# Runs of 1 to 16 small two-byte products between the tiles of the gate and up projection

## The chip, the cores and the metric

The kernel runs on one core of one Trainium2 chip. The metric is the device time of one execution in microseconds (us), smaller being better.

## The reference, cut to what matters

The reference is two transformer blocks on 256 tokens of width 1024. The first block has a mixer (latent attention beside a gated linear recurrence), a gated feed-forward layer and a gated embedding; the second has two attentions and a layer that picks experts by product keys. The change lies in the feed-forward layer of the first block:

```python
D_MODEL = 1024
D_FF = -(-8 * D_MODEL // (3 * 256)) * 256      # 2816
...
h = rms_norm(x, g_ffn[l])
x = x + (jax.nn.silu(h @ w_gate[l]) * (h @ w_up[l])) @ w_down[l]
gate = jax.nn.sigmoid(rms_norm(x, g_ple[l]) @ w_ple_gate[l])
x = x + gate * (p[l].astype(x.dtype) @ w_ple_proj[l])
```

`w_gate` and `w_up` are 1024 x 2816 each. The kernel holds them as one array `w_gu` of 44 units of 128 columns, a gate unit and an up unit in turn.

## The kernel before

**One product in three.** Weights and activations are float32, and each is split into a high part (`whi`, `hh`, of type fp32r) and a low rest (`wlo`, `hl`). A product is then the sum of three: high by high, high by rest, rest by high. `mm3s` (line 120) issues them: for one tile of `w_gu` it has 8 pieces of the inner dimension and three products of each, so 24 products of 128 x 128 weights with 256 tokens, 8 of each kind in a row, all added up in one PSUM bank of the pool `mm` (three buffers).

**One unit of weights.** `unit` (line 98) loads 512 KB of weights on SP's queue into `wraw`, ScalarE (ACT) rounds them to `whi` (L109), and VectorE (DVE) subtracts to get `wlo` (L114). `wraw`, `whi` and `wlo` have four buffers each, so the splits may run up to four units ahead of TensorE (PE).

**The tile loop.** `prodT` (line 133) walks over the units. For each 128 columns it takes a PSUM bank, calls `mm3s`, and then `emit` for the tile. With `pre` (here the two steps of the norm, `sums` at L234 and `spread` at L241, small products with `ones` and `ident`) the first emits are held back until the norm is there. `w_gu` is one call of `prodT` with 44 units. `emit_gu` scales a tile by the norm (L786, DVE); for a gate tile it takes SiLU (L789, ACT), and for an up tile it multiplies the two (L792, DVE) and splits the result into `acth` (L180, ACT) and `actl` (L181, DVE), which feed the products of `w_down` behind: 8 tiles of 66 products each. After these come the 48 products of `w_ple_proj`.

**The order.** The kernel is written for a tile framework that orders the instructions of each engine while it builds the program, from its own costs; each engine then runs its own list in order and waits on semaphores. PE, ACT, DVE, POOL (GpSimd) and SP have a list each.

**Another place with small products.** The experts' weights of the second block are spread to a table by products of one-hot float16 tiles (L1221): 8 or 16 products of 128 x 128 with 128 columns at a time, and between two such groups stand 24 wide products of L129, the same shape as a tile of `w_gu`.

Of the kernel before, what the change touches and what calls it, by code (L numbers as in the profile page):

```python
# [10 lines left out]
BF16 = mybir.dt.bfloat16  # L11
# [52 lines left out]
def body(tc, a, out, dbg=None):  # L64
    nc = tc.nc
    ctx = ExitStack()
    pool = lambda name, bufs=1, **k: ctx.enter_context(tc.tile_pool(name=name, bufs=bufs, **k))
# [8 lines left out]
    G = nc.gpsimd  # L76
    PE = nc.tensor

    def pmm():
        return ps.tile([128, 512], F32, name="mm", bufs=3)  # L80
# [4 lines left out]
    def tick(n):  # L85

        for g in list(sides):
            for _ in range(n):
                if next(g, "end") == "end":
                    sides.remove(g)  # L90
                    break
# [6 lines left out]
    def unit(ap, shape, pool=False, parts=1, between=None):  # L98


        n = int(np.prod(shape))
        raw = st.tile([128, 1024], F32, name="wraw", bufs=4)
        hi = st.tile([128, 1024], F32R, name="whi", bufs=4)
        lo = st.tile([128, 1024], F32R, name="wlo", bufs=4)
        ap = ap.rearrange("p a b -> p (a b)")
        for i in range(parts):
            s = slice(i * n // parts, (i + 1) * n // parts)
            nc.sync.dma_start(raw[:, s], ap[:, s])
            S.activation(hi[:, s], raw[:, s], AF.Copy)  # L109
            if pool == "add":  # L110
                S.activation(lo[:, s], raw[:, s], AF.Copy, scale=-1.0)
                G.dma_start(lo[:, s], raw[:, s], accum_op=OP.add)
            else:
                (G if pool else V).tensor_tensor(lo[:, s], raw[:, s], hi[:, s].bitcast(F32), op=OP.subtract)  # L114
            if between is not None:
                between(i)
        v = lambda t: t[:, :n].rearrange("p (a b) -> p a b", a=shape[0])
        return v(hi), v(lo)

    def mm3s(o, steps, x_late=False, fill=None, first=True, last=True):  # L120


        if x_late:
            order = [(i, j) for i in range(len(steps)) for j in range(3)]
        else:
            order = [(i, j) for j in (0, 2, 1) for i in range(len(steps))]
        for n, (i, j) in enumerate(order):
            wh, wl, xh, xl = steps[i]
            PE.matmul(o, (wh, wl, wh)[j], (xh, xh, xl)[j], start=first and n == 0, stop=last and n == len(order) - 1)  # L129
            if fill is not None and j == 2 and i < len(steps) - 1:  # L130
                fill()

    def prodT(name, n0, n1, kt, cols, x, emit, steps=0, pool=lambda u: False, pre=(), given=None, fill=None, behind=(), late=False):


        xh, xl = x
        held = []
        late = late or len(pre) > 0
        pre = list(pre)
        for u in range(n0, n1):  # L140
            wh, wl = given if given is not None and u == n0 else unit_behind(behind if u > n0 + 1 else (), a[name][u], (kt, cols), pool(u))
            for c in range(cols // 128):
                p = pmm()
                o = p[:, :T]
                s = slice(c * 128, (c + 1) * 128)
                first = late and u == n0 and c == 0
                mm3s(o, [(wh[:, k, s], wl[:, k, s], xh[:, k], xl[:, k]) for k in range(kt)], first, fill if first else None)
                held.append((u * (cols // 128) + c, o))
                if pre:
                    pre.pop(0)()  # L150
                if not pre:
                    for i in held:
                        emit(*i)
                    held = []
                tick(steps)

    def natural(p, wh, wl, x, j, kts, first, last, x0=0):
# [21 lines left out]
    def split(hi, lo, src):  # L179
        S.activation(hi, src, AF.Copy)  # L180
        V.tensor_tensor(lo, src, hi.bitcast(F32), op=OP.subtract)  # L181
# [6 lines left out]
    def unit_behind(behind, *args, **kw):  # L188

        with ExitStack() as order:  # L190
            for i in behind:
                order.enter_context(tc.issue_after(i.ins))
            return unit(*args, **kw)
# [54 lines left out]
    def show(name, ap):  # L248
        if dbg is not None and name in dbg:
            nc.sync.dma_start(dbg[name], ap)  # L250
# [22 lines left out]
    with tc.tile_pool(name="la", bufs=1) as la, tc.tile_pool(name="pa", bufs=1, space=PSUM) as pa:  # L273
# [425 lines left out]
        steps = nm1.make(pay)  # L699
# [8 lines left out]
        def emit_gz(j, p):  # L708
# [4 lines left out]
            G.tensor_tensor(gz[:, j], gz[:, j], rows[:, 128:640], op=OP.mult)  # L713

        prodT("w_in", 0, 4, 8, 128, h, emit_z, 4, pre=[steps[0], first_spread], given=unit0, pool=lambda u: u == 2, fill=busy)
        sides.append(tables())
        latent_stats()
        prodT("w_in", 4, 10, 8, 128, h, emit_z, 3, pool=lambda u: u > 4 and u % 2 == 1 and "add")
        ready.add(("z", 0))
        sides.extend([hgrn(), hgrn_out()])  # L720
# [19 lines left out]
        for j in range(2):  # L740
# [3 lines left out]
            S.activation(vm[:, j], pv, AF.Copy, scale=rc[:, 1, j:j + 1])  # L744
        sides.append(mla_k(pk))
        prodT("w_in", 10, 16, 8, 128, h, emit_z, 1, pool=lambda u: u % 2 == 1 and "add")
        ready.add(("z", 1))
        nat512("w_in_nat", 4, h, emit_gz, 4, pool=lambda q: q % 2 == 1 and "add")
# [28 lines left out]
    with tc.tile_pool(name="lf", bufs=1) as la, tc.tile_pool(name="pf", bufs=1, space=PSUM) as pf:  # L777
        pfx = lambda: pf.tile([128, 512], F32, name="fx", bufs=2)
        n1 = norm
        act = (la.tile([128, 22, T], F32R, name="acth"), la.tile([128, 22, T], F32R, name="actl"))  # L780
        hold = {}

        def emit_gu(n, o):
            f, up = n // 2, n % 2
            t = la.tile([128, T], F32, name=f"gu{up}", bufs=2)
            V.tensor_tensor(t, o, n1.r, op=OP.mult)  # L786
            if up == 0:
                s = la.tile([128, T], F32, name="gsi", bufs=2)
                S.activation(s, t, AF.Silu)  # L789
                hold[0] = s  # L790
            else:
                V.tensor_tensor(t, t, hold[0], op=OP.mult)  # L792
                split(act[0][:, f], act[1][:, f], t)

        prodT("w_gu", 0, 44, 8, 128, n1.h, emit_gu, pre=n1.make(pfx), behind=n1.last)
        x2 = xb()
        norm2 = Norm("g_ple")
        for n in range(8):
            p = pmm()
            for k0, k1 in ((0, 8), (8, 16), (16, 22)):  # L800
                wh, wl = unit(a["w_down"][n][:, k0:k1], (k1 - k0, 128))
                mm3s(p[:, :T], [(wh[:, k], wl[:, k], act[0][:, k0 + k], act[1][:, k0 + k]) for k in range(k1 - k0)],
                     n == 0 and k1 == 22, first=k0 == 0, last=k1 == 22)
            V.tensor_tensor(x2[:, n], x1[:, n], p[:, :T], op=OP.add)
            norm2.add(n, x2[:, n])
        show("x2", x2)

        pT = la.tile([128, 2, T], F32, name="pT")
        nc.sync.dma_start(pT, a["pT"])
        pR = (la.tile([128, 2, T], F32R, name="pRh"), la.tile([128, 2, T], F32R, name="pRl"))  # L810
        split(pR[0], pR[1], pT)
        pp = la.tile([128, 8, T], F32, name="pp")

        def emit_pp(n, o):
            S.activation(pp[:, n], o, AF.Copy, scale=0.5)

        prodT("w_ple_proj", 0, 2, 2, 512, pR, emit_pp)
        x3 = xa()
        norm = Norm("g_mix2")

        def emit_ple(n, o):
            t = la.tile([128, T], F32, name="gu0", bufs=2)
            V.tensor_tensor(t, o, norm2.r, op=OP.mult)
            S.activation(t, t, AF.Tanh, scale=0.5)
            V.scalar_tensor_tensor(t, t, 1.0, pp[:, n], op0=OP.add, op1=OP.mult)
            V.tensor_tensor(x3[:, n], x2[:, n], t, op=OP.add)
            norm.add(n, x3[:, n])

        prodT("w_ple_gate", 0, 8, 8, 128, norm2.h, emit_ple, pre=norm2.make(pfx), behind=norm2.last)
        show("x3", x3)  # L830
# [595 lines left out]
```

## Time and profile before

| | us |
|---|---|
| median of 3 runs | 1429.27 |
| lowest and highest of these | 1424.44 and 1433.63 |
| the profiled execution, its own time | 1428.57 |
| its span, first to last instruction | 1426.8 |

The profile is that of one execution. PE is the time of products, PEld that of loading their stationary operand, which overlaps. A row of the timeline gives the start, the time from the first start to the last end, the engine, the line, the operation, the tiles, the shape and how many instructions are merged in it; in brackets stands the idle time before it and what ended that. A product's own time is longer than the distance between two starts, since products overlap in the array; what a stream of products costs is read from the starts. Some product records are missing from the trace, so counts in a window can be a few per cent low.

### The profile page before, as it was taken

The page shows a single profiled execution, that of the slowest core. Times are in us where ns is not written, and L with a number is a line of the kernel's source. Part 1 is how long each engine was busy: PE and PEld are TensorE (multiplying, and loading weights), DVE is VectorE, ACT ScalarE, POOL GpSimd, SP SyncE. Part 2 cuts the span into 40 slices and gives each one's busy share as a digit, 9 for nine tenths or more (in the row PEclk, how much of TensorE's full clock was granted, in tenths as well). Part 3 has the DMA queues.
Part 4 walks back from the last instruction along what each step waited for, and adds up shares of the span by engine and source line. Part 5 has one row for each costly group of instructions (what it writes and reads, how often), then busy time and mean ns, then how long its engine had stood idle before and what let it go on. Part 6 is the DMA issues. An engine that isn't in the chain of part 4 may idle for free.

```text
span 1426.8 us, 25304 instructions
## 1 busy us (share of the span) xinstructions
PE 1396.8 (98%) x9962; PEld 1281.2 (90%) x9962; DVE 961.2 (67%) x1792; ACT 770.3 (54%) x1183; POOL 127.6 (9%) x118
## 2 busy tenths in 40 slices
PE   9899999999999999989999999999999999999997
PEld 9796899999979889989999999989999899888886
DVE  7866876666775557776978995655555555577775
ACT  6764655444655444654358885444445444444443
POOL 4322200001110000147300000000000000000000
PEclk9999999999999999999999999999999999999999
DMA  7662466566555334664468778777667776797652
GB/s 242 193 176 61 156 201 185 191 178 192 165 166 155 112 118 148 204 179 153 133 210 291 269 277 289 217 218 218 196 208 220 217 220 201 234 277 224 205 191 89
DMA packets 105143, 277.52 MB, mean 195 GB/s; under 512 B 8512, under 2 KB 42048, under 8 KB 102848
## 3 DMA queue, kind: packets, MB, share of 16 engines
q1 hardware_dynamic: 100848, 252.31, 56.9%
q10 hardware_dynamic: 2304, 16.78, 2.8%
q0 software_dynamic: 1872, 6.82, 2.6%
q8 instruction: 78, 1.28, 0.4%
q14 instruction: 41, 0.34, 0.1%
HBM read 251.23 MB, written 17.83 MB: 189 GB/s over the span
## 4 chain that ended last, share of the span: by engine, by line
PE 86%; DVE 4%; DMA 4%; ACT 2%; issue 2%; POOL 1%; POOLq 0%; SPq 0%; ACTq 0%; DVEq 0%
PE mm L129 47%; PE ax L1249 8%; PE ax L1251 8%; PE ax L1250 8%; PE mm L163 4%; PE ax L1221 2%; PE mm L1057 2%; DMA wlo<-wraw 1%; PE sc L919 1%; DVE wlo L114 1%; PE sc L129 1%; ACT whi L109 1%; PE ao L913 1%; DMA gd<-hl 1%; DMA wraw<-in_expert_u_dram 0%
## 5 line engine op out<-in xcount | busy, mean ns | idle before, releaser
L109 ACT ACTIVATE whi<-wraw 128x1024 fp32r<-128x1024 f32 (+3 forms) x445 | 456.8, 1031 | 479.5 <-PE mm L129 154.9
L114 DVE TENSOR_TENSOR wlo<-wraw,whi 128x1024 fp32r<-128x1024 f32 (+3 forms) x410 | 486.9, 1191 | 262.2 <-ACT whi L109 252.8
L129 PE MATMUL mm<-hh,whi 128*128 128x256 f32 x1912 | 279.5, 285 | 1.2 <-DVE xa L766 0.7
L129 PE MATMUL mm<-hh,wlo 128*128 128x256 f32 x1912 | 268.9, 280 | 6.5 <-DMA wlo<-wraw 3.6
L129 PE MATMUL mm<-hl,whi 128*128 128x256 f32 x1912 | 269.7, 280 | 1.2 <-DVE hl L186 1.0
L129 PEld LDWEIGHTS mm<-hh,whi 128*128 128x128 f32 x1912 | 249.9, 189 | 8.9 <-ACT whi L109 0.9
L129 PEld LDWEIGHTS mm<-hh,wlo 128*128 128x128 f32 x1912 | 242.7, 189 | 7.3 <-DMA wlo<-wraw 3.8
L129 PEld LDWEIGHTS mm<-hl,whi 128*128 128x128 f32 x1912 | 242.6, 189 | 2.3 <-DVE hl L186 2.2
L1249 PE MATMUL ax<-whi,al 128*128 128x512 f32 x512 | 202.8, 396 | 1.5 <-DVE al L181 1.5
L1251 PE MATMUL ax<-whi,ah 128*128 128x512 f32 x512 | 202.6, 396 | 0.0
L1250 PE MATMUL ax<-wlo,ah 128*128 128x512 f32 x512 | 202.3, 395 | 0.0
L1251 PEld LDWEIGHTS ax<-whi,ah 128*128 128x128 f32 x512 | 96.2, 188 | 23.0
L1249 PEld LDWEIGHTS ax<-whi,al 128*128 128x128 f32 x512 | 96.2, 188 | 22.0 <-issue 1.7
L1250 PEld LDWEIGHTS ax<-wlo,ah 128*128 128x128 f32 x512 | 96.3, 188 | 20.4
L1062 ACT ACTIVATE hs<-mm 128x256 f32<-128x256 f32 x128 | 47.5, 371 | 45.5 <-PE mm L129 28.6
L1265 POOL TENSOR_TENSOR ff<-fss 128x1 f32<-128x1 f32 x2 | 1.4, 700 | 723.3 <-ACT fsq L1260 723.3
L114 POOL TENSOR_TENSOR wlo<-wraw,whi 128x1024 fp32r<-128x1024 f32 x22 | 52.8, 2400 | 39.7 <-ACT whi L109 33.6
L181 DVE TENSOR_TENSOR al<-am,ah 128x256 fp32r<-128x256 f32 x128 | 53.4, 418 | 0.0
L180 ACT ACTIVATE ah<-am 128x256 fp32r<-128x256 f32 x128 | 51.4, 401 | 3.6 <-DVE am L1238 3.6
L786 DVE TENSOR_TENSOR gu<-mm,rbc 128x256 f32<-128x256 f32 x44 | 18.6, 424 | 39.4 <-PE mm L129 39.4
L1211 DVE TENSOR_TENSOR one<-iota,iab 128x2048 f16<-128x2048 f16 x32 | 39.0, 1220 | 2.0 <-PE ax L1221 2.0
L1214 DVE TENSOR_TENSOR oA<-one,g 128x2048 f16<-128x2048 f16 x32 | 39.1, 1225 | 1.0
(406 smaller groups left out, 1558.7 us busy)
## 6 DMA issues: line engine op xcount, KB each, us to landing
wraw<-in_expert_u_dram SPq DMA_DIRECT2D x128, 512.0 KB, 4.1
wraw<-in_expert_v_dram SPq DMA_DIRECT2D x128, 512.0 KB, 3.6
wraw<-in_w_gu_dram SPq DMA_DIRECT2D x44, 512.0 KB, 3.5
wraw<-in_w_in_nat_dram SPq DMA_DIRECT2D x24, 512.0 KB, 3.5
wraw<-in_w_down_dram SPq DMA_DIRECT2D x16, 512.0 KB, 3.6
wraw<-in_w_in_g_dram SPq DMA_DIRECT2D x16, 512.0 KB, 3.5
wraw<-in_w_pq_dram SPq DMA_DIRECT2D x16, 512.0 KB, 4.6
gd<-hh ACTq DMA_DIRECT2D x8, 1024.0 KB, 6.7
```

Of the source, the lines that this page charges most:

```text
L109: S.activation(hi[:, s], raw[:, s], AF.Copy)
L114: (G if pool else V).tensor_tensor(lo[:, s], raw[:, s], hi[:, s].bitcast(F32), op=OP.subtract)
L129: PE.matmul(o, (wh, wl, wh)[j], (xh, xh, xl)[j], start=first and n == 0, stop=last and n == len(order) - 1)
L163: PE.matmul(p, xs[:, x0 + k, s], w[:, k], start=first and i == 0 and k == 0, stop=last and i == 2 and k == kts - 1)
L180: S.activation(hi, src, AF.Copy)
L181: V.tensor_tensor(lo, src, hi.bitcast(F32), op=OP.subtract)
L1062: S.activation(t, p[:, :T], AF.Gelu)
L1211: V.tensor_tensor(one, iota[:, None].to_broadcast(s2), iab[:, qs].rearrange("p q w b -> p (q w) b")[:, :, None].to_broadcast(s2), op=OP.is ...
L1214: V.tensor_tensor(A2, ow[:, :, 0:1].to_broadcast(s3), g2[:, qs].rearrange("p q k b -> p (q k) b")[:, :, None].to_broadcast([128, PAIRS * 2 ...
L1249: PE.matmul(o, al[:, js], hi[:, ns], start=c == 0, stop=False)
L1250: PE.matmul(o, ah[:, js], lo[:, ns], start=False, stop=False)
L1251: PE.matmul(o, ah[:, js], hi[:, ns], start=False, stop=c == 127)
```

## The change

`prodT` gets a callback `then` that is called after each tile. In the call for `w_gu` it puts a run of small products on PE: each is a product of a bfloat16 tile of ones, 128 x 128, with itself, into 128 columns of a PSUM bank of its own (`between`, of the pool `fx`), which nothing reads. The table `runs` has one number for each of the 44 tiles: 28 of them are not zero, and they sum to 190.

```diff
-    def prodT(name, n0, n1, kt, cols, x, emit, steps=0, pool=lambda u: False, pre=(), given=None, fill=None, behind=(), late=False):
+    def prodT(name, n0, n1, kt, cols, x, emit, steps=0, pool=lambda u: False, pre=(), given=None, fill=None, behind=(), late=False, then=None):
...
                     held = []
+                if then is not None:
+                    then()
                 tick(steps)
...
-        prodT("w_gu", 0, 44, 8, 128, n1.h, emit_gu, pre=n1.make(pfx), behind=n1.last)
+        onesb = la.tile([128, 128], BF16, name="onesb")
+        G.memset(onesb, 1.0)
+        between = pfx()
+        runs = [0, 0, 1, 0, 2, 0, 3, 0, 4, 0, 5, 0, 6, 0, 7, 0, 8, 0, 9, 0, 10, 0, 11, 0, 12, 0, 8, 8, 12, 12, 4, 4, 1, 1, 2, 2, 3, 3, 16, 0, 8, 16, 12, 0]
+
+        def run_of_ones():
+            for _ in range(runs.pop(0)):
+                PE.matmul(between[:, 0:128], onesb, onesb, start=True, stop=True)
+
+        prodT("w_gu", 0, 44, 8, 128, n1.h, emit_gu, pre=n1.make(pfx), behind=n1.last, then=run_of_ones)
```

The built programs show where the new instructions stand. Lines behind the new code are higher by 2 or by 11 in the changed kernel. The first place is PE's list at the start of `w_gu`, from the second tile's step of the norm on; before it reads:

```order
L129 MATMUL mm<-hh,wlo 128x256 x8
L241 MATMUL fx<-cst,rnat 128x128 x2
L129 MATMUL mm<-hh,whi 128x256 x8
L129 MATMUL mm<-hl,whi 128x256 x8
L129 MATMUL mm<-hh,wlo 128x256 x8
L129 MATMUL mm<-hh,whi 128x256 x8
```

and in the changed kernel, from the second of these tiles to the second run:

```order
L129 MATMUL mm<-hh,wlo 128x256 x8
L804 LDWEIGHTS onesb
L804 MATMUL fx<-onesb 128x128
L129 MATMUL mm<-hh,whi 128x256 x8
L129 MATMUL mm<-hl,whi 128x256 x8
L129 MATMUL mm<-hh,wlo 128x256 x8
L129 MATMUL mm<-hh,whi 128x256 x8
L129 MATMUL mm<-hl,whi 128x256 x8
L129 MATMUL mm<-hh,wlo 128x256 x8
L804 LDWEIGHTS onesb
L804 MATMUL fx<-onesb 128x128
```

Each small product is a load of weights and a product of its own; the wide products around it keep their order, and the list has 190 such pairs in all.

The second place is POOL's list around the end of the mixer. `onf` belongs to the mixer's last norm, and `sqa` and `rnat` to the norm ahead of `w_gu`; before:

```order
L713 TENSOR_TENSOR gz<-gz,rows 128x512 x2
L198 TENSOR_TENSOR onf_1676<-onf_1677,mhalf 128x4
L198 TENSOR_TENSOR onf_1694<-onf_1695,mhalf 128x4
L223 TENSOR_TENSOR sqa<-sq 128x256
L223 TENSOR_TENSOR sqa<-sqa,sq 128x256 x5
```

and in the changed kernel:

```order
L715 TENSOR_TENSOR gz<-gz,rows 128x512 x2
L200 TENSOR_TENSOR onf_1676<-onf_1677,mhalf 128x4
L200 TENSOR_TENSOR onf_1694<-onf_1695,mhalf 128x4
L798 MEMSET onesb 128x128
L225 TENSOR_TENSOR sqa<-sq 128x256
L225 TENSOR_TENSOR sqa<-sqa,sq 128x256 x5
```

The memset of `onesb` went in ahead of the norm's sums. Its memory belonged to tiles of the mixer, so it waits for them, the last being the mixer's transposes on PE (L533 before).

The third place is DVE's list at the 28th tile of `w_gu`, from where on the two programs differ to near the end of the loop; before:

```order
L181 TENSOR_TENSOR actl<-gu_2994,acth 128x256
L786 TENSOR_TENSOR gu_3065<-mm,rbc 128x256
L114 TENSOR_TENSOR wlo<-wraw,whi 128x1024
L792 TENSOR_TENSOR gu_3065<-gu_3065,gsi 128x256
L786 TENSOR_TENSOR gu_3101<-mm,rbc 128x256
L114 TENSOR_TENSOR wlo<-wraw,whi 128x1024
L181 TENSOR_TENSOR actl<-gu_3065,acth 128x256
```

and in the changed kernel:

```order
L183 TENSOR_TENSOR actl<-gu_3075,acth 128x256
L788 TENSOR_TENSOR gu_3154<-mm,rbc 128x256
L114 TENSOR_TENSOR wlo<-wraw,whi 128x1024
L794 TENSOR_TENSOR gu_3154<-gu_3154,gsi 128x256
L183 TENSOR_TENSOR actl<-gu_3154,acth 128x256
L788 TENSOR_TENSOR gu_3198<-mm,rbc 128x256
L114 TENSOR_TENSOR wlo<-wraw,whi 128x1024
```

The step that makes `actl` moved up, from behind the next tile's scaling and split to right behind the product of gate and up; on ACT `acth` moved up by one split of weights in the same way. SP's list is the same in both.

## Rows read from the trace of the kernel before

**Rows 1.** The page: busy time of the engines.

```profile
PE 1396.8 (98%) x9962; PEld 1281.2 (90%) x9962; DVE 961.2 (67%) x1792; ACT 770.3 (54%) x1183; POOL 127.6 (9%) x118
```

**Rows 2.** Windows: start:end, length, busy us by engine (x count), clock, DMA share, GB/s.

```profile
181.50:302.20 120.70, 120.70 (x1028) 120.70 (x1027) 81.25 (x130) 61.53 (x87) 0.00 (x0) 1.00 0.62 191
302.20:368.00 65.80, 65.80 (x561) 65.77 (x560) 38.80 (x43) 33.90 (x49) 5.18 (x6) 1.00 0.66 190
```

**Rows 3.** Waits in w_gu: who waited for whom, us, times, longest.

```profile
ACT whi L109 <- PE mm L129: 55.0, 40, 1.8
DVE gu L786 <- PE mm L129: 39.4, 42, 1.2
```

**Rows 4.** Timeline of PE inside w_gu, wide products in groups of eight.

```profile
250.36 1.10 PE L129 MATMUL mm<-hl,whi 128*128 128x256 f32 x8
251.30 1.11 PE L129 MATMUL mm<-hh,wlo 128*128 128x256 f32 x8
...
254.13 1.11 PE L129 MATMUL mm<-hh,wlo 128*128 128x256 f32 x8
```

**Rows 5.** Timeline of PE: 16 small products of L1221 among wide ones.

```profile
791.54 1.07 PE L129 MATMUL mm<-hh,wlo 128*128 128x256 f32 x8
792.45 1.09 PE L1221 MATMUL ax<-oA,one 128*128 128x128 f16 x16
793.35 1.18 PE L129 MATMUL mm<-hh,whi 128*128 128x256 f32 x8
794.37 1.07 PE L129 MATMUL mm<-hl,whi 128*128 128x256 f32 x8
795.27 1.07 PE L129 MATMUL mm<-hh,wlo 128*128 128x256 f32 x8
```

**Rows 6.** The same with 8 small products.

```profile
860.96 1.07 PE L129 MATMUL mm<-hh,wlo 128*128 128x256 f32 x8
861.87 0.63 PE L1221 MATMUL ax<-oA,one 128*128 128x128 f16 x8
862.31 1.19 PE L129 MATMUL mm<-hh,whi 128*128 128x256 f32 x8
863.33 1.10 PE L129 MATMUL mm<-hl,whi 128*128 128x256 f32 x8
864.28 1.10 PE L129 MATMUL mm<-hh,wlo 128*128 128x256 f32 x8
```

**Rows 7.** The same with 16, behind slower wide products.

```profile
816.88 1.10 PE L129 MATMUL mm<-hh,wlo 128*128 128x256 f32 x8
817.83 1.09 PE L1221 MATMUL ax<-oA,one 128*128 128x128 f16 x16
...
819.74 1.07 PE L129 MATMUL mm<-hl,whi 128*128 128x256 f32 x8
820.65 1.07 PE L129 MATMUL mm<-hh,wlo 128*128 128x256 f32 x8
```

**Rows 8.** Loads of the small products, by line: ns min/median/max.

```profile
L1221 PEld LDWEIGHTS <-one x512: 96/97/103, 734.2 to 862.2; 128*128 128x128 f16 x171
```

**Rows 9.** The mixer's last transposes, by line: duration, first and last start.

```profile
L533 PE MATMUL ax<-cst,on x8: 270/273/328, 149.0 to 154.4; 128*128 128x128 f32 x8
```

**Rows 10.** Timeline of POOL ahead of w_gu.

```profile
150.12 1.01 POOL L198 TENSOR_TENSOR onf<-onf,mhalf 128x4 f32<-128x4 f32 x1 [2.60 <-DVE onf L197]
166.36 0.94 POOL L223 TENSOR_TENSOR sqa<-sq 128x256 f32<-128x256 f32 x1 [15.23 <-ACT sq L218]
```

**Rows 11.** Timeline of DVE: the scaling of two tiles that follow each other.

```profile
252.44 0.42 DVE L786 TENSOR_TENSOR gu<-mm,rbc 128x256 f32<-128x256 f32 x1 [0.94 <-PE mm L129]
...
255.27 0.42 DVE L786 TENSOR_TENSOR gu<-mm,rbc 128x256 f32<-128x256 f32 x1 [0.93 <-PE mm L129]
```

**Rows 12.** Timeline of ACT beside it.

```profile
251.55 1.06 ACT L109 ACTIVATE whi<-wraw 128x1024 fp32r<-128x1024 f32 x1 [1.77 <-PE mm L129]
252.51 0.40 ACT L180 ACTIVATE acth<-gu 128x256 fp32r<-128x256 f32 x1
```

## The prediction

> **What bounds the kernel now.** I read the page first: PE is busy for 98% of the span [rows 1], so it is products that the time consists of. Then the stage of the change. From the second tile of `w_gu` to its end PE is busy for all of 120.70 us, and in `w_down` behind it for all of 65.80 us, at a granted clock of 1.00, the 2.4 GHz level [rows 2]. The waits there run the other way: ACT waits for PE before it may split the next unit, 55.0 us in 40 waits, and DVE waits for PE's tiles, 39.4 us in 42 waits; no wait of PE is listed [rows 3]. So whatever is put into PE's list in `w_gu` lies on the path, and what it delays (all else of the program depends on `w_gu`) has no slack to give it back.
>
> Next, the pace of PE's stream. In `w_gu` four groups of eight wide products start within 3.77 us, from 250.36 to 254.13 [rows 4]: 0.94 us for a group, 118 ns for a product, 2.83 us for a tile. In the stage with small float16 products, groups of the same shape start 0.91 or 0.90 us apart [rows 5]: 113.5 ns for a product, 0.10 us less for a tile. Both stretches have the same clock and no idle time in between, so PE's stream has two paces, and `w_gu` runs at the slow one. This decides the sign of a small term below.
>
> **The 190 products.** Each is a load of 128 columns of weights and a product with 128 columns, both of a two-byte type. The nearest rows are the small products of L1221: the same shape and width of type, float16 for bfloat16, with wide products of L129 on both sides. Sixteen of them start at 792.45 and the wide ones go on at 793.35: 0.90 us [rows 5]. Eight start at 861.87 and the wide ones go on at 862.31: 0.44 us [rows 6]. Eight more cost 0.46 us, 57.5 ns each. 190 x 57.5 ns = 10.9 us.
>
> **The 28 runs.** The wide group behind a run takes 1.02 us (793.35 to 794.37) where its neighbours take 0.91: a restart of 0.11 us. From that comes off what the 57.5 ns count too much: 16 x 57.5 = 920 ns against the 900 measured, 8 x 57.5 = 460 against 440. This leaves 0.09 us for a run of either length. No row has a run of fewer than eight; I take the same 0.09 us, since the restart is of the wide products and not of the small ones. 28 x 0.09 = 2.5 us. Together with the products: 13.4 us.
>
> Bounds for this. From below: nothing here can go beside the stream, as PE has no idle time; a run of one could at least cost its product without the restart, so 10.9 us. From above: the load of a small product takes 97 ns [rows 8], and it is hidden now behind the product ahead of it; if in this run of equal operands it were not, a product would cost at least these 97 ns, 190 x 97 ns = 18.4 us and 20.9 us with the restarts. I take the 57.5 ns, as its rows have the shape, the type and the neighbours.
>
> The Trainium skill, page "TensorE: Matmul & The Clock Gate", section "Back-to-back issue gap", says that in a real stream of loads and products one of 128 columns takes about 81 ns, and by the distance of single products about 56. The row of 16 in 0.90 us agrees with the latter. By the 81 ns the products would be 15.4 us, a rival below.
>
> **The pace behind a run.** A run does more than take its time: it sets the pace of the wide products behind it. Behind eight small ones the stream that was fast (0.91 us a group) goes on slowly, at 0.95 us from 863.33 on [rows 6]. Behind sixteen it is fast both when it was fast before [rows 5] and when it was slow (0.95 us ahead, 0.91 behind) [rows 7]. Without a disturbance the pace stays: it is the same in all of `w_gu`. So each run may turn the slow stream into a fast one until the next run, and the last run sets the pace of `w_down` as well. What counts are 41 tiles behind the first run at 0.10 us each. By the rows for eight and sixteen, 3 of these tiles (behind the two runs of 16) become fast, 0.3 us, and 5 (behind the four runs of 8) stay slow. For runs of 1 to 7 and 9 to 12 there is no row: 32 tiles, up to 3.3 us, and, behind the last run of 12, the last tile and the 528 products of `w_down` and 48 of `w_ple_proj`, 600 x 4.3 ns = 2.6 us. Either way lies between nothing and 5.9 us; with no reason for one of them I take half, 2.9 us. With the 0.3 us the paces give back 3.2 us.
>
> **What is hidden.** The memset of `onesb` stands in POOL's list ahead of the sums of the norm. It waits for the mixer's transposes, whose last starts at 154.4 [rows 9]; POOL then has nothing to do until 166.36 [rows 10]. Eleven microseconds cover it; if that cover were gone, the sums, and with them PE's step of the norm, would come later by the memset's own length. The new order on DVE in the second half of the loop makes DVE wait for `acth` on ACT, which takes 0.40 us, or 1.06 us more if a split stands ahead of it [rows 12]. DVE is idle for 0.93 us of every tile's 2.83 [rows 11], and the splits run up to four units ahead, so this costs nothing; if the cover were gone, PE would wait for `wlo`, up to 0.5 us (1.46 less 0.93) for each of the at most nine pairs of tiles left, 4.5 us. Loads stay in their order and have more time than before.
>
> **Sum.** 10.9 + 2.5 - 3.2 = 10.2 us. The profiled execution took 1428.57 us, 1.8 more than its span, and becomes 1438.8. It lies 0.7 below the median of the three runs, so I put the sum on the median: 1429.27 + 10.2 = 1439.5, a ratio of 1.007. What a measurement of this kernel can tell from no change is about 1%, 14.3 us.
>
> **The rivals.**
>
> *The small products cost their loads.* Equal operands for load and product, one array of ones read on both sides, are in no row; if they keep a load from running beside the product ahead of it, the sum is 20.9 us at 97 ns, and the paces, which are decided behind the runs, give back 3.2: 17.7 us, 1447.0, slower by over 1%. It ends on that side from a price of (14.3 - 2.5 + 3.2) / 190 = 79 ns on. Against it: the float16 rows hide loads of the same length for 8 and 16 in a row [rows 5, 6]. Chance 7%.
>
> *Half of the loads are hidden.* A load runs beside the product ahead of it only every other time, so a product costs the middle of 57.5 and 97 ns, 77 ns: 14.7 + 2.5 - 3.2 = 14.0 us, 1443.3, at the edge of 1%. Against it speak the same rows. Chance 5%. The section of the skill named above comes to nearly this: by its 81 ns the sum would be 14.7 us. The trace agrees with its other figure.
>
> *The new order starves PE.* The waits of DVE for `acth` come through in full: 10.2 + 4.5 = 14.7 us, 1444.0, over 1%. Against it: the four units of lead, and that DVE waits for PE and not the other way. Chance 3%.
>
> *All unknown runs leave the stream fast.* 13.4 - 6.2 = 7.2 us, 1436.5. *None of them does.* 13.4 - 0.3 = 13.1 us, 1442.4. These are the ends of the forecast itself: for them speaks that the pace behind a run is the same each time for one length; between them nothing in the trace chooses.
>
> *The change doesn't do what it says.* Products that nothing reads cost nothing, because they are dropped or fall in gaps: 1429.3. PE's list has all 190, and PE has no gaps there. Chance 2%. Were the fast pace to carry on beyond `w_ple_proj` as well, it would be within the forecast's lower end, since the next steps of a norm set the pace anew.
>
> **How the numbers follow.** The forecast (products at 57.5 ns, restarts, paces in part) has 83%, with a time of 1436.5 to 1442.4 by the paces alone. The three runs of before lie up to 4.8 us from their median, so a median of some runs may be off by 3: 1433.5 to 1445.5. With the lower half of the price rivals the range is 1434 to 1446; about 8 in 10 lie in it. Slower by over 1% (above 1443.6): 7% of the first rival, 3% and 2% of the two at the edge, and 6% of the forecast by the spread of runs, 18%. Faster by over 1%: no mechanism gives it, 1%. Within 1%: 81%.
>
> **What would show it.** In the changed kernel's trace the stretch from the first run to the end of `w_gu` holds 190 pairs of load and product of L804, 57 or 58 ns apart inside a run, and the wide group behind each run takes about 0.1 us more than the next. Between runs groups of eight take 0.94 or 0.91 us; which of them should go by the length of the run, the same length giving the same pace each time (1, 2, 3, 4, 8 and 12 occur more than once), with 8 slow and 16 fast. PE still has no wait of its own in `w_gu`. `w_down` shows one pace throughout. Wrong would be: small products 80 ns apart or more, a restart that grows with the length of the run or is over 0.2 us, waits of PE for `wlo` in the second half of the loop, or a length whose pace changes from run to run.

## The result, and the profile after

The changed kernel takes 1438.05 us, the median of 15 runs (1434.31 to 1441.06); the kernel before takes 1425.42 us beside it, in 15 runs (1420.68 to 1433.63). The ratio is 1.0072, with a 95% interval of 1.0055 to 1.0089: 0.7% slower, clear of the noise, but inside the 1% that the prediction called no change. The quotient of the two medians is higher, 1.0089 (12.6 us), at the upper end of that interval. The forecast was 1439.5 us and a ratio of 1.007. The profiled execution of the changed kernel took 1437.46 us, with a span of 1435.7, 8.9 us longer than that of the profile before.

The page of the changed kernel, busy time by engine; the line answers to [rows 1].

```profile
PE 1409.2 (98%) x10152; PEld 1293.3 (90%) x10152; DVE 963.0 (67%) x1792; ACT 771.0 (54%) x1183; POOL 128.0 (9%) x119
```

PE has 190 products more, and its busy time grew by 12.4 us. The next view is the windows of the changed kernel: first the loop of `w_gu` from the tile behind the norm's second step to its last product, then the products of `w_down`. It answers to [rows 2], whose first window ran 1.9 us into `w_down`.

```profile
179.34:308.30 128.96, 128.96 (x1202) 127.87 (x1201) 80.32 (x127) 61.51 (x87) 0.00 (x0) 1.00 0.57 177
308.30:370.49 62.19, 62.19 (x531) 62.19 (x530) 37.18 (x41) 29.65 (x40) 5.13 (x6) 1.00 0.63 189
```

The same two stretches of the kernel before, which the experiments below come back to, in the same view:

```profile
181.49:300.29 118.80, 118.80 (x1011) 118.80 (x1010) 79.55 (x127) 61.16 (x87) 0.00 (x0) 1.00 0.61 190
300.29:362.48 62.19, 62.19 (x530) 62.19 (x529) 37.23 (x41) 29.65 (x40) 5.18 (x6) 1.00 0.66 191
```

The loop grew by 10.16 us with PE busy for all of it at a clock of 1.00, and `w_down` by nothing. That the span grew by 8.9 us only lies outside: `w_gu` began 2.15 us earlier (179.34 against 181.49), and what stands behind `w_down` took 0.9 us more. The waits of the changed kernel from 182.2 to 308.3 us, which answer to [rows 3], again name no wait of PE; three of the rows:

```profile
ACT whi L109 <- PE mm L129: 51.3, 35, 1.9
DVE gu L788 <- PE mm L129: 42.9, 39, 2.1
...
DVE actl L183 <- ACT acth L182: 3.4, 7, 0.5
```

The last row is the wait of DVE for `acth` that the prediction had named; it came seven times and stayed hidden.

All instructions of the new line, by duration in ns (min/median/max); they answer to [rows 8].

```profile
L804 PEld LDWEIGHTS <-onesb x190: 96/98/100, 182.2 to 305.3; 128*128 128x128 bf16 x190
L804 PE MATMUL fx<-onesb x190: 219/219/230, 182.3 to 305.4; 128*128 128x128 bf16 x190
```

The timeline of PE in the changed kernel shows what a run costs: a run of 1, the first run of 8, a run of 12 with a run of 8 behind it, and a run of 16.

```profile
182.25 0.23 PE L804 MATMUL fx<-onesb 128*128 128x128 bf16 x1
182.29 1.19 PE L129 MATMUL mm<-hh,whi 128*128 128x256 f32 x8
183.32 1.07 PE L129 MATMUL mm<-hl,whi 128*128 128x256 f32 x8
184.23 1.07 PE L129 MATMUL mm<-hh,wlo 128*128 128x256 f32 x8
...
223.12 0.62 PE L804 MATMUL fx<-onesb 128*128 128x128 bf16 x8
223.55 1.19 PE L129 MATMUL mm<-hh,whi 128*128 128x256 f32 x8
224.57 1.10 PE L129 MATMUL mm<-hl,whi 128*128 128x256 f32 x8
225.52 1.11 PE L129 MATMUL mm<-hh,wlo 128*128 128x256 f32 x8
...
247.58 0.84 PE L804 MATMUL fx<-onesb 128*128 128x128 bf16 x12
248.23 1.19 PE L129 MATMUL mm<-hh,whi 128*128 128x256 f32 x8
249.25 1.10 PE L129 MATMUL mm<-hl,whi 128*128 128x256 f32 x8
...
253.97 0.62 PE L804 MATMUL fx<-onesb 128*128 128x128 bf16 x8
254.40 1.16 PE L129 MATMUL mm<-hh,whi 128*128 128x256 f32 x8
255.39 1.07 PE L129 MATMUL mm<-hl,whi 128*128 128x256 f32 x8
256.30 1.07 PE L129 MATMUL mm<-hh,wlo 128*128 128x256 f32 x8
...
291.40 1.07 PE L804 MATMUL fx<-onesb 128*128 128x128 bf16 x16
292.27 1.16 PE L129 MATMUL mm<-hh,whi 128*128 128x256 f32 x8
293.27 1.07 PE L129 MATMUL mm<-hl,whi 128*128 128x256 f32 x8
```

Read the starts. Sixteen products take 0.87 us (291.40 to 292.27) and eight 0.43, so eight more cost 0.44: 55 ns each by these rows, 55.8 by the starts in ns (877 less 430), near the 57.5 of [rows 5, 6]. Behind each run the first wide group takes about 0.1 us more than the next. The pace behind the run of 1 is fast (0.91 us from 183.32 to 184.23), behind 12 slow. Behind 8 it is slow the first time (0.95 us from 224.57 to 225.52) and fast the second time (0.91 us from 255.39 to 256.30), though a slow stream stood ahead of both. The prediction had named this as a sign of being wrong.

### The profile page after: what moved, and what is told of

It reads as the page before. It is cut to its first block, busy times and chain, and to the rows that moved or that the text cites. A ratio compares the mean times of both kernels' runs of the same rounds, so it can differ in the third digit from the quotient of the medians.

```text
span 1435.7 us, 25689 instructions
## 1 busy us (share of the span) xinstructions
PE 1409.2 (98%) x10152; PEld 1293.3 (90%) x10152; DVE 963.0 (67%) x1792; ACT 771.0 (54%) x1183; POOL 128.0 (9%) x119
## 4 chain that ended last, share of the span: by engine, by line
PE 86%; DVE 4%; DMA 3%; ACT 3%; issue 2%; POOL 1%; SPq 0%; POOLq 0%; ACTq 0%; DVEq 0%
PE mm L129 47%; PE ax L1260 8%; PE ax L1262 8%; PE ax L1261 8%; PE mm L165 3%; PE ax L1232 2%; PE mm L1068 2%; DVE wlo L114 1%; PE sc L930 1%; ACT whi L109 1%; PE sc L129 1%; PE fx L804 1%; PE ao L924 1%; DMA wlo<-wraw 1%; DMA gd<-hl 1%
```

## The experiments

What was to be settled: whether the price is by the product and by the run, as in the prediction's sum, or whether runs are free or dear in another way; and what sets the pace. The table gives the time of each kernel. "Loop" is `w_gu` from the tile behind the norm's second step to the first product of `w_down`, as in the windows above; `w_down` is the stretch behind it, to `w_ple_proj`. The third tile is the first of the loop; the prediction and the expectations of the second profiles call it the second. A ratio and its interval are given where there were several runs.

| kernel | us, median (runs) | loop | `w_down` |
|---|---|---|---|
| before, profile above | 1425.42 (15) | 118.80 | 62.19 |
| changed, profile above | 1438.05 (15) | 128.96 | 62.19 |
| table of zeros | 1426.24 (12) | 114.33 | 62.19 |
| one run of 1 | 1427.26 (12) | 114.60 | 62.19 |
| 28 runs of 1 | 1431.29 (12) | 119.00 | 62.19 |
| one run of 190, at the end | 1433.78 (6) | 124.93 | 59.93 |
| runs of 1 at both ends | 1425.87 (12) | 114.64 | 62.27 |
| ones of four bytes | 1446.62 (4) | 136.17 | 62.19 |
| 8, 4 and 12 repeated | 1441.88 (1) | 127.24 | 62.19 |
| before again | 1427.07 (1) | 114.34 | 62.19 |
| table of zeros again | 1428.63 (1) | 118.80 | 62.19 |
| changed again | 1435.73 (1) | 128.96 | 62.19 |
| one run of 16, at the end | 1428.47 (1) | 115.22 | 62.27 |
| lengths 8 apart | 1440.21 (1) | 130.94 | 62.19 |

The kernel before took 1426.92 us (29 runs) beside the first four, 1426.71 (17) beside the next three, and 1430.56 or 1430.59 (1 each) beside the last five.

**Everything but the products.** The memset, the callback and the new order of DVE and ACT stay; the table is all zeros.

```diff
-        runs = [0, 0, 1, 0, 2, 0, 3, ..., 8, 16, 12, 0]
+        runs = [0] * 44
```

> All 44 numbers of the table are 0: the memset of ones stays, no small product is left. My theory (56 ns a product, 0.08 us a run, and the pace that a run leaves): no time of its own, 0 us against before, and the loop of w_gu takes 118.8 us as before, at the slow pace. Rival (memset and the new order of the lists have a price): the loop or the norm ahead of it is longer by some us.

Ratio 0.9999 (0.9978 to 1.0020): all that is not a product costs nothing within the interval, 0.2% or 3 us. But the loop took 114.33 us, 4.47 less than in the profile of before, with the same products in it. That was not foreseen, and is taken up by the second profiles below, where equal paces are compared.

**One run of one product.**

```diff
+        runs = [0, 0, 1] + [0] * 41
```

> One product alone, behind the third tile. In the changed kernel the stream was fast behind all three runs of one. My theory: 0.13 us for the run, and all wide products behind it up to the next norm, 41 tiles and 600 less 24 more, go at 113.3 instead of 117.8 ns: 1560 x 4.4 ns = 6.9 us less; the loop of w_gu takes 114.6 us, w_down 59.8 instead of 62.2, the whole 6.8 us less than before, 1418.6. Rival (time goes by products alone, 53 ns each, and the pace is no matter of the run): +0.05 us, 1425.5, loop 118.9.

Ratio 1.0001 (0.9981 to 1.0021). The loop is 0.27 us above that of the table of zeros: 0.17 for the run and 0.10 for the one tile ahead of it, which ran slowly. So the loop was as my theory had it (114.6 us), but `w_down` stayed slow (62.19 against 59.8 forecast), and the 6.8 us less of the forecast did not come. In this execution the run did turn a stream fast that had entered slow, but a gain of 2 us, half of the 4.47, would not show in this interval.

**28 runs of one.**

```diff
+        runs = [min(x, 1) for x in [0, 0, 1, 0, 2, 0, 3, ..., 8, 16, 12, 0]]
```

> The same 28 runs, each of one product: 28 products instead of 190. My theory: 28 x (0.056 + 0.078) = 3.75 us, less the fast pace behind every run of one, 6.9 us: 3.1 us less than before, the loop of w_gu 118.2 us, w_down 59.8. Rival (products alone): 28 x 0.053 = +1.5 us, loop 120.3, w_down 62.2. A third (no price per run, but the pace): 1.6 - 6.9 = -5.3 us.

Ratio 1.0036 (1.0019 to 1.0052). Against the table of zeros, with the stream fast throughout in both, 28 runs cost 4.67 us in the loop, 0.167 each. One product explains 0.056 of that; the rest, 0.11, is the restart. So even the shortest run pays for it, and runs without a restart are excluded. The forecast of 3.1 us less failed: the kernel is slower, since the base was read as slow, the restart is dearer than 0.078 us for a run of one, and `w_down` stayed slow.

**One run of 190.** The same 190 products, all behind the last tile.

```diff
+        runs = [0] * 43 + [190]
```

> All 190 products in one run behind the last tile, none elsewhere. My theory: 190 x 55.8 ns + 0.08 us = 10.7 us ahead of w_down, the loop otherwise slow as before (129.5 us with the run), and w_down slow or fast by a length that I have not seen, 0 or 2.5 us off: +10.7 or +8.2 us. Rival (a product costs 64 ns, nothing per run): +12.1 us. A rival by which a long run costs more for each product: over 11 us in the run itself.

Ratio 1.0067 (1.0043 to 1.0091). The timeline of PE around the run in this kernel:

```profile
295.77 10.78 PE L804 MATMUL fx<-onesb 128*128 128x128 bf16 x190
306.36 1.16 PE L129 MATMUL mm<-acth,whi 128*128 128x256 f32 x8
307.36 1.07 PE L129 MATMUL mm<-actl,whi 128*128 128x256 f32 x8
308.26 1.07 PE L129 MATMUL mm<-acth,wlo 128*128 128x256 f32 x8
```

From 295.77 to 306.36 are 10.59 us, 55.7 ns for a product; there is no sign of the 97 ns of its load. The loop missed its forecast of 129.5 us, because it ran at the fast pace in this execution: 114.3 us and the run. This is also the only kernel in which `w_down` goes fast: 0.90 us from 307.36 to 308.26, and 59.93 us in all against 62.19.

**Runs of one at both ends.** If a short run leaves the stream fast, one right ahead of `w_down` should speed it up.

```diff
+        runs = [0, 0, 1] + [0] * 40 + [1]
```

> Two products: one behind the third tile, one behind the last. So far the loop of w_gu was slow or fast by itself, three executions each, and turned slow at the first product of w_down in all but the kernel that had its 190 ones right ahead of it. My theory, mended so: the first run holds the loop fast, 114.6 us, the second keeps w_down fast, 59.9 us instead of 62.2; against before, whose loop is 118.8 or 114.3, 2.0 us less on the mean by the loop and 2.3 by w_down, less 0.1: some 4 us less, 1422.7. Rival (w_down's pace comes from its own operands, and only the long run got past that): w_down 62.2, 1.9 us less, 1425.0.

Ratio 1.0001 (0.9984 to 1.0018), and `w_down` slow, 62.27 us. The idea that a run's length alone decides what the next stretch does fell here. The 4 us less of my theory did not come; the 1.9 us less of the rival lie inside the interval.

**Ones of four bytes.** The table of the change, with the ones in the wide products' own type.

```diff
-        onesb = la.tile([128, 128], BF16, name="onesb")
-        G.memset(onesb, 1.0)
+        onesb = la.tile([128, 128], F32R, name="onesb")
+        S.activation(onesb, ones, AF.Copy)
```

> The table of the change with ones of type fp32r, that of the wide products, in place of bfloat16. If the restart of 0.078 us is the change of type: no restart, and if a four-byte load of 128 columns sets the distance, 113 ns a product: 190 x 0.113 = 21.5 us over a slow or fast loop, 140.3 or 135.8 us. If the restart is the change from narrow to wide and a product is paid by its columns: 56 ns and 0.078 us a run, 12.8 us, loop 131.6 or 127.1 less the paces, as in the change.

Ratio 1.0124 (1.0086 to 1.0161). The timeline of PE around a run of 12 and a run of 4 in this kernel:

```profile
271.27 1.45 PE L804 MATMUL fx<-onesb 128*128 128x128 f32 x12
272.56 1.14 PE L129 MATMUL mm<-hh,whi 128*128 128x256 f32 x8
273.54 1.07 PE L129 MATMUL mm<-hl,whi 128*128 128x256 f32 x8
274.44 1.07 PE L129 MATMUL mm<-hh,wlo 128*128 128x256 f32 x8
275.35 0.55 PE L804 MATMUL fx<-onesb 128*128 128x128 f32 x4
275.75 1.14 PE L129 MATMUL mm<-hh,whi 128*128 128x256 f32 x8
```

The run takes 1.29 us (271.27 to 272.56), twice the 0.65 of the run of 12 in two-byte type. The run of 4 takes 0.40 us (275.35 to 275.75), so eight more products cost 0.89, 111.7 ns each by the starts in ns, nearly as much as a wide product of 113.3; its loads, with a median of 192 ns, are about as long as those of the wide ones (188 ns). That the load sets the price here fits but was not tried apart. What is left for the restart is about 0.02 us: the loop exceeds 114.33 by 21.8 us; less 190 x 111.7 ns = 21.2 and the 0.1 of the slow tile ahead of the first run, 0.5 remain for 28 runs. So the 0.08 us of the two-byte runs go with the change of type; the change from 128 to 256 columns, which is in this kernel too, does not bring them. That is the first reading of the expectation, with its loop of 135.8 us. The stream is fast behind all 28 runs.

**The same length again and again.**

```diff
+        runs = [0, 0, 0] + [8, 0] * 7 + [4, 0] * 7 + [12, 0] * 6 + [0]
```

> Runs of 8 seven times, of 4 seven times, of 12 six times, with two tiles (48 wide products) behind each. If the length alone sets the pace: one pace for all of a length, 4 and 12 slow, and 8 all alike. If the stream's own place at the entry has a say (in the changed kernel 8 left it slow once and fast three times): the first of a length may differ, and then each repeats what the one before gave. Price by my theory, whatever the paces: 156 x 55.8 ns + 20 x 0.078 = 10.3 us.

8 left the stream fast 7 times of 7, 4 slow 7 of 7, 12 slow 6 of 6. So a length does have a pace of its own when it is repeated, and the first run of 8 in the changed kernel is an exception that needs a reason.

**Second profiles of three kernels.** Nothing is edited; the question is whether a pace belongs to the program or to one execution of it.

> The kernel of before, for a second profile of it. Theory A: the pace at which w_gu runs without products is not the program's but the execution's; it is set where the second step of the norm (two transposes between the first and the second tile) turns the pace of the first tile into the other one. Then this execution may show the loop, from the second tile to the first product of w_down, at 118.8 us (0.94 us a group) or at 114.3 us (0.91), whichever is the opposite of the first tile's pace. Rival B: the pace belongs to the program, and before is always slow: 118.8 us again. Time by both 1424 to 1434 us.

> The changed kernel with a table of zeros, for a second profile. Theory A (the pace of w_gu belongs to the execution): the loop takes 114.3 us as in the first profile or 118.8 us, the opposite of the first tile's pace. Rival B (it belongs to the program, which has a memset and another order on DVE and ACT): 114.3 us again. Between them the two kernels without products separate A from B if either of them shows a time that it did not show before. Time by both 1423 to 1431 us.

> The changed kernel itself, for a second profile. Theory A (a run turns or keeps the pace according to what was before it as well as to its length): the prices of the products, 55.8 ns, and of the restart, 0.08 us, come again to within 1 ns and 0.01 us; the paces behind the runs may differ for some lengths, 8 above all (slow once and fast three times in the first profile), so the loop takes 128 to 131 us. Rival B (the pace behind a run is fixed by the list of instructions): the same paces behind the same runs, the first run of 8 slow and the other three fast, and the loop at 128.9 to 129.0 us. Time by both 1434 to 1441 us.

The loop of the kernel before in its second profile:

```profile
181.20:295.54 114.34, 114.34 (x1011) 114.34 (x1010) 79.53 (x127) 61.15 (x87) 0.00 (x0) 1.00 0.63 197
```

and the loop of the table of zeros in its second profile:

```profile
180.80:299.60 118.80, 118.80 (x1011) 118.80 (x1010) 79.55 (x127) 61.16 (x87) 0.00 (x0) 1.00 0.61 189
```

The two kernels have changed places: theory A held for both. At equal pace their loops agree within 0.01 us, 118.80 with 118.80 and 114.34 with 114.33, so memset and new order cost the loop nothing. The chip does not choose the pace either: on each of the three chips on which the experiments ran, some loops were entered slow and some fast. The unchanged kernel runs its loop in 118.80 or in 114.34 us, at the same clock with PE busy throughout. What tells the two apart stands just ahead of it. The timeline of PE around the norm's second step, first profile of before:

```profile
180.22 1.07 PE L129 MATMUL mm<-hh,wlo 128*128 128x256 f32 x8
181.13 0.60 PE L241 MATMUL fx<-cst,rnat 128*128 128x128 f32 x4
...
182.52 1.10 PE L129 MATMUL mm<-hl,whi 128*128 128x256 f32 x8
183.46 1.11 PE L129 MATMUL mm<-hh,wlo 128*128 128x256 f32 x8
```

and second profile of before:

```profile
179.90 1.11 PE L129 MATMUL mm<-hh,wlo 128*128 128x256 f32 x8
180.84 0.61 PE L241 MATMUL fx<-cst,rnat 128*128 128x128 f32 x4
...
182.21 1.07 PE L129 MATMUL mm<-hl,whi 128*128 128x256 f32 x8
183.11 1.07 PE L129 MATMUL mm<-hh,wlo 128*128 128x256 f32 x8
```

A fast tile (0.91 us for the group from 180.22 to 181.13) comes out slow behind the norm's step, and a slow one (0.94, from 179.90) comes out fast. This held in all 14 profiles, seven times each way. The changed kernel's second profile gave the loop of 128.96 us again, with the same pace behind each of the 28 runs, the first run of 8 slow and the others fast; that is what the rival forecast, by which the list of instructions fixes these paces. But both profiles entered the loop at the same pace, and theory A then gives the same, so these two do not tell the theories apart for this kernel.

**A run of 16 ahead of w_down.**

```diff
+        runs = [0] * 43 + [16]
```

> The changed kernel with one run alone, of 16 products, behind the last tile (table 43 times 0, then 16). Theory A: a run sets the pace of w_down if it is long, and a run of 16 leaves a stream fast wherever it stood: w_down at 59.9 us, as behind a run of 190. Rival B: w_down falls into the slow pace within its first 20 products whatever stands ahead of it, a run of 190 excepted: 62.2 us. The run itself 16 x 55.8 ns + 0.08 us = 0.97 us by both; time 1426 to 1430 us (A up to 2.3 less than B).

The rival was right: `w_down` is slow at once, 0.94 us from the second group to the third.

```profile
296.01 1.07 PE L804 MATMUL fx<-onesb 128*128 128x128 bf16 x16
296.89 1.19 PE L129 MATMUL mm<-acth,whi 128*128 128x256 f32 x8
297.92 1.10 PE L129 MATMUL mm<-actl,whi 128*128 128x256 f32 x8
298.86 1.10 PE L129 MATMUL mm<-acth,wlo 128*128 128x256 f32 x8
```

**Lengths that are 8 apart.** A pattern in the runs so far: 1 and 9, 2 and 10, 3 and 11 leave a fast stream, 4 and 12 a slow one. Lengths that had not been tried test it.

```diff
+        runs = [0, 0, 5, 0, 13, 0, 21, 0, 6, 0, 14, 0, 22, 0, 7, 0, 15, 0, 1, 0, 17, 0, 2, 0, 18, 0, 3, 0, 19, 0, 4, 0, 20, 0, 8, 0, 24, 0, 12, 0, 10, 0, 0, 0]
```

> The changed kernel with 20 runs of other lengths in w_gu, two tiles between them: 5, 13, 21, 6, 14, 22, 7, 15, 1, 17, 2, 18, 3, 19, 4, 20, 8, 24, 12, 10, 241 products in all. Theory C, read off the runs so far: lengths that differ by 8 leave the same pace (1 and 9, 2 and 10, 3 and 11 fast, 4 and 12 slow, 8 and 16 fast with one exception). Then 13, 21, 17, 18, 19, 24, 10 leave the stream fast like 5, 1, 2, 3, 8 and 2, and 14, 22, 15, 20, 12 slow like 6, 7 and 4. Loop: 114.3 us for the fast stream + 241 x 55.8 ns + 20 x 0.08 us + 8 slow pairs of tiles (behind 6, 14, 22, 7, 15, 4, 20, 12) at 0.21 us = 131.0 us. Rival D: the length alone chooses, short runs either way and all of 13 and more fast like 16; only 6, 7, 4 and 12 are slow, 130.2 us. Time by both 1438 to 1444 us.

13, 17, 18, 19, 21 and 24 left a fast stream, 14, 20 and 22 a slow one, as forecast. One missed: 15 left it fast. The timeline of PE behind 14 and behind 15 in this kernel:

```profile
208.13 0.96 PE L804 MATMUL fx<-onesb 128*128 128x128 bf16 x14
208.89 1.19 PE L129 MATMUL mm<-hh,whi 128*128 128x256 f32 x8
209.92 1.10 PE L129 MATMUL mm<-hl,whi 128*128 128x256 f32 x8
210.86 0.40 PE L129 MATMUL mm<-hh,wlo 128*128 128x256 f32 x2
...
227.70 1.01 PE L804 MATMUL fx<-onesb 128*128 128x128 bf16 x15
228.53 1.17 PE L129 MATMUL mm<-hh,whi 128*128 128x256 f32 x8
229.54 1.07 PE L129 MATMUL mm<-hl,whi 128*128 128x256 f32 x8
230.44 1.07 PE L129 MATMUL mm<-hh,wlo 128*128 128x256 f32 x8
```

Behind 14 a group takes 0.94 us (209.92 to 210.86), behind 15 0.90. The rival, by which all long runs leave a fast stream, fell at 14, 20 and 22. Both exceptions seen in `w_gu`, this 15 and the first 8 of the changed kernel, are the next run after a run of 7. Each did what a run four products longer or shorter does (15 like 3, 11 and 19; 8 like 4 and 12); why a 7 should leave that behind was not tried.

## Why the prediction was right

**The bound and the cover held.** PE stayed fully busy and had no wait of its own, and at equal pace the loop of the table of zeros is as long as that of before, to 0.01 us. The memset ran at 153.22 us for 0.20, and POOL was idle for 10.71 us behind it, so the cover was there. DVE did wait for `acth`, 3.4 us in seven waits of at most 0.5, and no wait of PE came of it. The starved PE and the change that does nothing fell.

**The products: 10.9 us forecast, 10.6 measured.** 190 x 55.7 ns, by the run of 190. The float16 rows were the right neighbours. Both rivals on the load (97 and 77 ns) fell. Of the two figures of the Trainium skill, page "TensorE: Matmul & The Clock Gate", section "Back-to-back issue gap", about 81 and about 56 ns, the trace agrees with the 56 again, for equal operands too.

**The restarts: 2.5 us forecast, 2.3 measured.** The loop of 128.96 us exceeds the fast one of the table of zeros by 14.6; less 10.6 for products and 1.7 for 16 slow tiles (0.105 each), 2.3 remain, 0.083 for a run. It does not grow with the length: 0.11 for a run of 1, and 0.09 for the 190 (306.36 to 307.36 took 1.00 us where the next group took 0.90 or 0.91).

**The paces: 3.2 us forecast, 2.7 measured, but not by the step as put.** Behind the runs 26 of the loop's 42 tiles were fast, 0.105 us each. The forecast took half of an unknown, and that it came near is luck. Of its 32 unknown tiles 20 were fast, 2.1 us; `w_down`, from which it took half of 2.6 us, gave nothing. And "8 slow and 16 fast" with "the same length giving the same pace each time" failed, one of the signs of being wrong that the prediction had named: 8 is fast but for one time. The other signs did not show. Rows of two places [rows 6, 7] were too few to give a length its pace.

**The step that failed is the base.** "Without a disturbance the pace stays: it is the same in all of `w_gu`" was right of one execution, and the prediction read it as a property of the kernel; by it, it chose the sign of the term of the paces. The loop of before takes 118.80 or 114.34 us, and the changed one took 128.96 us both times. So the change costs 10.2 us in the loop against the first kind of execution and 14.6 against the second. Against the fast kind the runs give nothing back: the slow tiles that they bring cost 1.7. In the whole program this is hard to see: the spans of the two profiles of before differ by 1.5 us (1426.8 and 1425.3), not by 4.5, since what stands behind `w_down` took 1064.3 us in the first and 1067.6 in the second. In the two profiles of the changed kernel, with equal loops, it took 1065.2 and 1061.9, so it varies by some us of its own; whether it has to do with the pace of `w_gu` is not shown. Of the 14 profiles seven came out of the norm's step at either pace; if both kinds are equally common, the mean is 12.4 us, an estimate from these two. The measured 0.72%, 10.3 us with an interval of 7.8 to 12.7, allows 10.2 as well as 12.4, and the medians, 12.6 us apart, lie nearer to the latter. So that the forecast of 10.2 came so close to the ratio is partly luck: it was made from a profile that showed the slow kind.

**Still open:** why two paces exist, why the step in the pace goes by eights, why a 7 shifts the next run, and why `w_down` starts slowly except behind the 190. There the rule by eights does not hold: 190 has a remainder of 6 and left `w_down` fast, while 1 and 16 left it slow.

## What to carry to other kernels

On an engine that is busy throughout, put a price on every instruction that is added, and take it from the nearest rows of the same shape and type: here 56 ns for a small two-byte product and 0.08 us for each change of type, right to 2 ns and 0.01 us in the mean over all runs. Before gains of a few tenths of a per cent are read from the pace of a stream, take a second profile of the unchanged kernel: here its own two executions differed by 4.5 us in the stage of the change. A pace that a run of small products brings was no lever here: no kernel tried was measurably faster than the one before. The kernels whose loop was held fast by a run of one came out at 1.0001; a gain of 2 us in the mean, half of the 4.5, would lie inside their intervals.

## What the runs showed that was not expected

Wide four-byte products, 128 x 128 with 256 columns, go at 113.3 or 117.8 ns with PE busy and the granted clock at 1.00 in both cases; behind the norm's four transposes the pace was the other one in all 14 profiles. Inside `w_gu` the pace behind a run of two-byte products goes by its length in steps of eight, in 46 of 48 runs of the two tables that mix lengths: with a remainder of 0, 1, 2, 3 or 5 fast, of 4, 6 or 7 slow. Narrow products with four-byte loads cost 111.7 ns, twice the 55.8 of two-byte ones with the same number of columns.
